# A mean over rows: the first load with 4 rows per partition, as eight DMAs of every eighth partition

## The chip, the cores and the metric

The kernel runs on one core of one Trainium2 chip. The metric is device time in microseconds. Most executions of a kernel agree within 0.3%. A kernel is profiled in one further execution, whose page and trace are quoted below; the durations there are of that execution.

## The reference

```python
batch, seq, dim = 32, 512, 1024
"x": np.random.randn(batch, seq, dim).astype(np.float32),
"divisor": float(dim),

def reference(x, divisor):
    return (np.sum(x, axis=-1) / divisor).astype(np.float32)
```

There are 16384 rows of 1024 float32 values, 67.1 MB; each row gives one mean.

## The kernel before

Each of the 128 partitions of the on-chip memory takes 128 whole rows: 16 from a first block of the input (`x_first`, L150), 96 from a main block (`x_main`), and 16 from a last block (`x_last`). Within a block the rows of one partition are contiguous, so n rows per partition are one piece of n x 4 KB for each partition. The blocks are cut into loads by the lists at L158 to L160. A pair is (rows per partition, how many of these rows ScalarE sums):

- first: 2 rows, then 14, all summed on VectorE
- main: five times 14 rows, then 14 (4 of them on ScalarE) and 12 (5 on ScalarE)
- last: 9, 4 and 2 rows and one row in two halves, `pa` and `pb`

All loads are issued by one engine, SyncE (SP), at L182, in program order, and each is one DMA over all 128 partitions. The tiles `t` of the first and main blocks, and the 9-row tile, rotate through a pool of three buffers (`bulk`, L166). A load into a used buffer waits on SP for the load that filled it and for the sums that read it. VectorE sums a tile with one instruction (L205, `TENSOR_REDUCE`) over all of its rows that aren't ScalarE's; ScalarE takes one row per instruction (L186). GpSimd multiplies the sums by 1/divisor (L207). The last rows are summed one at a time (L192). SP stores three results, at L223, L224 and L228.

Each DMA signals that it has landed on one of eight semaphores, which the framework deals out in turn (101, 102 and 104 to 109 in the trace); the ninth load has the first one's again.

Three helpers edit the finished program. `start_loads_at_once` (L19) takes the loads at the head of SP's list that wait for nothing and puts them into the first block, ahead of the barrier that all engines pass at the entry; it stops at the first load that has a wait. In the kernel before these are three loads: 2, 14 and 14 rows. `latest_wait_first` (L50) sorts the waits of an instruction that has several. `close_while_storing` (L69) lets the closing work run beside the last store.

Of the kernel before, what the change touches and what calls it, by code (L numbers as in the profile page):

```python
# [125 lines left out]
@with_exitstack  # L126
def kernel(
    ctx: ExitStack,
    tc: tile.TileContext,
    x: bass.AP,  # L130
    divisor: float,
    out: bass.AP,
):
    nc = tc.nc
    landed = nc.alloc_semaphore("landed")
    nc.at_finalize(start_loads_at_once)
    nc.at_finalize(latest_wait_first)
    nc.at_finalize(lambda nc: close_while_storing(nc, landed))
    xf = x.flatten_outer_dims()
    N, D = xf.shape  # L140
    P = nc.NUM_PARTITIONS
    scale = 1.0 / float(divisor)
    J = N // P
    assert J * P == N


    F, L = 16, 16
    M = J - F - L
    W = M + L
    x_first = bass.AP(tensor=x.tensor, offset=0, ap=[[F * D, P], [D, F], [1, D]])  # L150
    x_main = bass.AP(tensor=x.tensor, offset=P * F * D, ap=[[W * D, P], [D, M], [1, D]])
    x_last = bass.AP(tensor=x.tensor, offset=P * F * D + M * D, ap=[[W * D, P], [D, L], [1, D]])
    o_first = bass.AP(tensor=out.tensor, offset=0, ap=[[F, P], [1, F]])
    o_main = bass.AP(tensor=out.tensor, offset=P * F, ap=[[W, P], [1, M]])
    o_last = bass.AP(tensor=out.tensor, offset=P * F + M, ap=[[W, P], [1, L]])


    first = [(2, 0), (14, 0)]  # L158
    main = [(14, 0)] * 5 + [(14, 4), (12, 5)]
    last = [(9, 4), (4, 2), (2, 1)]  # L160
    assert sum(n for n, _ in first) == F
    assert sum(n for n, _ in main) == M and sum(n for n, _ in last) == L - 1

    pad = ctx.enter_context(tc.tile_pool(name="pad", bufs=1))
    pad.tile([P, 224], F32, name="pad")
    bulk = ctx.enter_context(tc.tile_pool(name="bulk", bufs=3))  # L166
    one = ctx.enter_context(tc.tile_pool(name="one", bufs=1))
    psum = ctx.enter_context(tc.tile_pool(name="junk", bufs=4, space=bass.MemoryType.PSUM))


    c = 512
    t4 = one.tile([P, 4, D], F32, name="t4")
    t2 = one.tile([P, 2, D], F32, name="t2")
    pa = one.tile([P, 768], F32, name="pa")[:, :c]
    pb = one.tile([P, D - c + 16], F32, name="pb")[:, : D - c + 2]
    res0 = one.tile([P, F], F32, name="res0")
    res = one.tile([P, M], F32, name="res")
    fin = one.tile([P, L], F32, name="fin")
    nc.gpsimd.memset(pb[:, D - c :], 0.0)  # L179

    def load(dst, src):
        tc.keep_in_program_order(nc.sync.dma_start(out=dst, in_=src))  # L182

    def act_sum(dst, src, by=1.0):
        junk = psum.tile([P, D], F32, name="junk")
        nc.scalar.activation(junk, src, COPY, scale=by, accum_out=dst)  # L186

    def dve_mean(dst, src, by=scale):


        h = src.shape[-1] // 2
        nc.vector.tensor_tensor_reduce(  # L192
            out=src[:, :h], in0=src[:, :h], in1=src[:, h:], scale=by, scalar=0.0,
            op0=ADD, op1=ADD, accum_out=dst,
        )

    for loads, src, dst in ((first, x_first, res0), (main, x_main, res)):
        j = 0
        for rows, on_act in loads:
            t = bulk.tile([P, 14, D], F32, name="t")  # L200
            load(t[:, :rows, :], src[:, j : j + rows, :])
            d = rows - on_act
            for i in range(d, rows):
                act_sum(dst[:, j + i : j + i + 1], t[:, i, :])
            nc.vector.reduce_sum(out=dst[:, j : j + d], in_=t[:, :d, :], axis=AX)  # L205
            j += rows
        nc.gpsimd.tensor_scalar_mul(out=dst, in0=dst, scalar1=scale)  # L207
    j = 0
    for rows, on_act in last:
        t = bulk.tile([P, 14, D], F32, name="t")[:, :rows, :] if rows > 4 else t4 if rows == 4 else t2  # L210
        load(t, x_last[:, j : j + rows, :])
        d = rows - on_act
        for i in range(rows):
            if i < d:
                dve_mean(fin[:, j + i : j + i + 1], t[:, i, :])
            else:
                act_sum(fin[:, j + i : j + i + 1], t[:, i, :], by=scale)
        j += rows
    load(pa, x_last[:, j, :c])
    load(pb[:, : D - c], x_last[:, j, c:])  # L220


    tc.keep_in_program_order(nc.sync.dma_start(out=o_first, in_=res0))  # L223
    tc.keep_in_program_order(nc.sync.dma_start(out=o_main, in_=res))  # L224

    dve_mean(pb[:, D - c : D - c + 1], pa, by=1.0)
    dve_mean(fin[:, j:], pb)
    tc.keep_in_program_order(nc.sync.dma_start(out=o_last, in_=fin))  # L228
# [35 lines left out]
```

## Time and profile before

| | |
|---|---|
| median of 3 runs | 160.52 us (160.48 to 160.53) |
| the profiled execution | 160.33 us |
| its span | 159.0 us |
| mean DMA rate over the span | 422 GB/s |
| 14-row load, issue to landing | 35.6 us (median of seven) |
| VectorE sum of 14 rows, 128x14336 | 15.09 us, six times |
| VectorE waits for loads, L205 | 34.0 us in nine waits, the longest 14.6 |

A span runs from the first to the last instruction of the profile, and the execution's own time has 1.33 us around it. The engines are DVE (VectorE), ACT (ScalarE), POOL (GpSimd) and SP (SyncE); a q behind a name is the engine's instruction queue. A row of the timeline has start and duration in us, engine, line, operation, output and input, and in brackets the idle time before it with what ended it. A row of the windows view has a stretch of time, its length, each engine's busy time with instructions, the clock, the busy share of the DMA engines and their rate. The bytes and the time of a packet are counted where the packet begins, so that a rate over a very short stretch can lie above what the engines can do.

### The profile page before, as it was taken

How to read it: one execution, taken by the hardware profiler on the slowest of the kernel's cores; microseconds unless marked ns; L12 is line 12 of the kernel's file. 1: busy time of each engine (PE TensorE's matmuls, PEld its weight loads, DVE VectorE, ACT ScalarE, POOL GpSimd, SP SyncE). 2: the span in 40 equal slices, each digit the busy share in tenths (PEclk: the TensorE clock that was granted, in tenths of full speed). 3: DMA queues.
4: the chain of work that ended last, by engine and by line, in shares of the span. 5: the costliest groups of instructions: out<-in, count | busy, mean ns of one | idle time of the engine just before them, and what ended most of it. 6: DMA issues, size and time to landing. Idle time of an engine off the chain costs nothing.

```text
span 159.0 us, 148 instructions
## 1 busy us (share of the span) xinstructions
DVE 117.2 (74%) x29; ACT 18.5 (12%) x33; POOL 1.0 (1%) x7
## 2 busy tenths in 40 slices
DVE  0500059995999599978999599959995996395643
ACT  3000000000000000000000000000000900390684
POOL 0000000000000000000000000000000000001000
DMA  7999999959999999699999999699999999999894
GB/s 278 447 462 462 462 462 462 462 260 433 462 462 462 462 462 462 303 390 462 462 462 462 462 462 404 303 447 462 462 462 429 396 396 408 482 445 445 350 420 169
DMA packets 2448, 67.18 MB, mean 422 GB/s; under 512 B 656, under 2 KB 656, under 8 KB 912
## 3 DMA queue, kind: packets, MB, share of 16 engines
q1 hardware_dynamic: 2448, 67.18, 98.3%
HBM read 67.11 MB, written 0.07 MB: 422 GB/s over the span
## 4 chain that ended last, share of the span: by engine, by line
DMA 77%; DVE 21%; SPq 1%; issue 0%; DVEq 0%
DMA t<-in_x_dram 56%; DMA pb<-in_x_dram 21%; DVE res L205 20%; SPq L182 1%; DVE pb L192 0%; DVEq L259 0%
## 5 line engine op out<-in xcount | busy, mean ns | idle before, releaser
L205 DVE TENSOR_REDUCE res<-t 128x14 f32<-128x14336 f32 (+3 forms) x9 | 111.2, 12360 | 34.0 <-DMA t<-in_x_dram 34.0
L186 ACT ACTIVATE junk<-t 128x1024 f32<-128x1024 f32 x16 | 16.2, 1013 | 136.8 <-DMA t<-in_x_dram 136.8
L192 DVE CUSTOM_DVE_ANT_0 t<-t 128x512 f32<-128x512 f32 x8 | 5.1, 688 | 6.1 <-DMA t<-in_x_dram 6.1
L186 ACT ACTIVATION_READ_ACCUMULATOR junk<-t 128x1 f32 x16 | 3.0, 186 | 0.0
L207 POOL TENSOR_SCALAR res<-res 128x16 f32<-128x16 f32 (+1 forms) x2 | 0.7, 352 | 143.3 <-DVE res L205 143.3
L186 ACT ACT_TABLE_LOAD x1 | 1.3, 1283 | 1.7 <-PEq L245 1.7
L192 DVE DVE_READ_ACCUMULATOR2_ANT fin<- 128x1 f32 x9 | 0.7, 82 | 0.0
L192 DVE CUSTOM_DVE_ANT_0 pb<-pb 128x257 f32<-128x257 f32 x1 | 0.4, 428 | 0.2 <-DMA pb<-in_x_dram 0.2
L192 DVE CUSTOM_DVE_ANT_0 pa<-pa 128x256 f32<-128x256 f32 x1 | 0.4, 426 | 0.0
L179 POOL MEMSET pb<- 128x2 f32 x1 | 0.1, 99 | 1.3 <-POOLq L245 1.3
L245 POOL MEMSET const-bfloat16-1.0<- 128x1 bf16 x1 | 0.1, 101 | 0.0
L245 POOL MEMSET const-uint8-127<- 128x1 uint8 x1 | 0.1, 101 | 0.0
L245 POOL MEMSET const-float32-0.0<- 128x1 f32 x1 | 0.1, 98 | 0.2 <-issue 0.2
L245 POOL MEMSET const-float32-1.0<- 128x1 f32 x1 | 0.1, 98 | 0.0
L192 DVE DVE_READ_ACCUMULATOR2_ANT pb<- 128x1 f32 x1 | 0.1, 84 | 0.0
## 6 DMA issues: line engine op xcount, KB each, us to landing
t<-in_x_dram SPq DMA_DIRECT2D x7, 7168.0 KB, 35.6
t<-in_x_dram SPq DMA_DIRECT2D x1, 6144.0 KB, 33.3
t<-in_x_dram SPq DMA_DIRECT2D x1, 4608.0 KB, 27.2
t<-in_x_dram SPq DMA_DIRECT2D x2, 1024.0 KB, 19.2
t<-in_x_dram SPq DMA_DIRECT2D x1, 2048.0 KB, 31.7
pa<-in_x_dram SPq DMA_DIRECT2D x1, 256.0 KB, 33.8
pb<-in_x_dram SPq DMA_DIRECT2D x1, 256.0 KB, 33.9
out_dram<-res SPq DMA_DIRECT2D x1, 48.0 KB, 11.6
```

The lines of the kernel that those rows point to most:

```text
L179: nc.gpsimd.memset(pb[:, D - c :], 0.0)
L182: tc.keep_in_program_order(nc.sync.dma_start(out=dst, in_=src))
L186: nc.scalar.activation(junk, src, COPY, scale=by, accum_out=dst)
L192: nc.vector.tensor_tensor_reduce(out=src[:, :h], in0=src[:, :h], in1=src[:, h:], scale=by, scalar=0.0, op0=ADD, op1=ADD, accum_out=dst,)
L205: nc.vector.reduce_sum(out=dst[:, j : j + d], in_=t[:, :d, :], axis=AX)
L207: nc.gpsimd.tensor_scalar_mul(out=dst, in0=dst, scalar1=scale)
L245: nc = _bacc.Bacc("TRN2", target_bir_lowering=False, num_devices=1)
```

## The change

The first load takes 4 rows per partition, and the second 12. The 4-row load is issued as eight DMAs. DMA number e, from 0 to 7, covers partitions e, 8 + e, 16 + e and so on up to 120 + e: sixteen partitions, one piece of 16 KB in each. All eight write the same tile, and VectorE's sum reads it as before. No other load has 4 rows in this loop; the 4-row load of the last block is issued elsewhere.

```diff
-    first = [(2, 0), (14, 0)]
+    first = [(4, 0), (12, 0)]
     main = [(14, 0)] * 5 + [(14, 4), (12, 5)]
     last = [(9, 4), (4, 2), (2, 1)]
...
             t = bulk.tile([P, 14, D], F32, name="t")
-            load(t[:, :rows, :], src[:, j : j + rows, :])
+            if rows == 4:
+
+                for e in range(8):
+                    load(t[e::8, :rows, :], src[e::8, j : j + rows, :])
+            else:
+                load(t[:, :rows, :], src[:, j : j + rows, :])
             d = rows - on_act
```

## The prediction

> **What bounds the kernel now.** I read the page first, for its span, busy shares and queues.
>
> ```profile
> span 159.0 us, 148 instructions
> DVE 117.2 (74%) x29; ACT 18.5 (12%) x33; POOL 1.0 (1%) x7
> q1 hardware_dynamic: 2448, 67.18, 98.3%
> DMA 77%; DVE 21%; SPq 1%; issue 0%; DVEq 0%
> ```
>
> No engine is busy beyond 74%, while the DMA queue's packets fill 98.3% of the sixteen DMA engines' time. The DVE 21% in the chain of waits is a buffer being read before its next load is issued; whether that costs anything is answered by the timeline of DVE.
>
> ```profile
> 4.63 2.29 DVE L205 TENSOR_REDUCE res<-t 128x2 f32<-128x2048 f32 x1 [4.63 <-DMA t<-in_x_dram]
> 21.51 15.09 DVE L205 TENSOR_REDUCE res<-t 128x14 f32<-128x14336 f32 x1 [14.59 <-DMA t<-in_x_dram]
> 38.44 15.09 DVE L205 TENSOR_REDUCE res<-t 128x14 f32<-128x14336 f32 x1 [1.84 <-DMA t<-in_x_dram]
> ...
> 123.10 10.82 DVE L205 TENSOR_REDUCE res<-t 128x10 f32<-128x10240 f32 x1 [1.88 <-DMA t<-in_x_dram]
> ...
> 157.10 0.43 DVE L192 CUSTOM_DVE_ANT_0 pb<-pb 128x257 f32<-128x257 f32 x1 [0.17 <-DMA pb<-in_x_dram]
> ```
>
> Each reduction starts when its tile lands. From 21.51 to 123.10 lie six tiles of 14 rows: 101.59/6 = 16.93 us for 7,340,032 bytes, or 433.5 GB/s, 27.1 per DMA engine. At that rate the input of 67.11 MB takes 154.8 us and the first two rows 2.42. The first tile lands at 4.61, so the stream has an effective start at 4.61 - 2.42 = 2.19; 2.19 + 154.8 = 157.0, and the last piece is indeed summed from 157.10. There is no gap anywhere in the load stream. So each microsecond lost or won by the stream at its start reaches the end, and nothing else does. The start itself is in the windows view and SP's timeline.
>
> ```profile
> core 0: us, DVE busy (x) ACT busy (x) POOL busy (x), PEclk, DMA share, GB/s
> 0.00:1.00 1.00, 0.00 (x0) 0.00 (x0) 0.19 (x4) 1.00 0.00 0
> 1.00:1.25 0.25, 0.00 (x0) 0.00 (x0) 0.00 (x0) 1.00 2.25 360
> 1.25:1.50 0.25, 0.00 (x0) 0.00 (x0) 0.00 (x0) 1.00 0.62 98
> 1.50:1.75 0.25, 0.00 (x0) 0.01 (x1) 0.01 (x1) 1.00 0.43 131
> 1.75:2.00 0.25, 0.00 (x0) 0.25 (x1) 0.09 (x1) 1.00 0.50 197
> 2.00:2.25 0.25, 0.00 (x0) 0.25 (x1) 0.00 (x0) 1.00 0.80 328
> 2.25:2.50 0.25, 0.00 (x0) 0.25 (x1) 0.00 (x0) 1.00 1.16 492
> ```
> ```profile
> 0.00 1.34 SPq L182 DMA_DIRECT2D t<-in_x_dram  x3
> ```
>
> [...]Nothing moves in the first microsecond; the sixteen engines begin between 1.0 and 1.75 us, and the full rate is there only from 2.25. The packet records say the same: first packets begin at 1.02 to 1.68, take 0.31 to 1.01 us where a later 8 KB packet takes 0.309, and the sixteen engines are done with the tile at 3.87 to 4.28; the landing follows 0.33 later. An engine that began at 1.02 and ran at the full rate would be done at 3.44. So the ramp costs the slowest engine 4.28 - 3.44 = 0.84 us: all that the change can win there.
>
> [...]
>
> **The change part by part.** The sum is made on the profiled execution: 160.33 us, span 159.0, 1.33 around it; the median of the runs is 160.52, so 0.19 is added at the end.
>
> *SP's queue.* Seven issues are added ahead of the rest. The three at the start follow each other by some 0.47 us (1.34 for three), so eight end at about 3.8. Eight DMA semaphores are dealt in turn: the second load is the ninth DMA and gets the first one's again. The store at L224, in the same position in the kernel before, has an event wait of its own on the load that last had its semaphore, so I expect the second load to wait for the first small DMA, the third load for the second. A load with a wait is not moved to the start by L19, so it comes after the entry barrier: 0.33 us after the last early issue in before (1.34 to the barrier's end at 1.67), so here at about 4.1, its packets at 5.1 to 5.8. The small DMAs keep the engines fed till 5.9 at least (1.02 + 4.84), so this is hidden; if the stream were faster by a microsecond it would show. Behind SP in the barrier wait the ACT table load (1.74) and a memset: first needed at 123 and 157 us, nothing.
>
> *The packets.* Each engine gets eight packets of 16 KB and eight of 48 KB where it had eight of 8 KB and eight of 56 KB: as many, the same bytes. Seven more semaphore packets at 6 ns each in the packet records: +0.04. Small DMAs queued one behind the other cost nothing more by themselves: pb lands 33.9 + 123.14 = 157.04, pa 33.8 + 122.64 = 156.44, 0.60 for 256 KB, the full rate.
>
> *DVE.* Reductions cost 1.067 us a row and 0.15 each (from 15.09 for 14 and 2.29 for 2): 4.42 for 4 rows, 12.95 for 12, together as before. It sat idle 14.59 us in this stretch. The buffer of tile 0 comes free later, but its next load's bytes aren't due before 38 us. Nothing.
>
> *The ramp.* With one packet per engine in the first DMA the engines could all begin near 1.02 and the loss of 0.84 shrink. But first packets that began late (1.55 to 1.68) were done at about the same moment as the early ones, 2.0[...]. From 0 to 0.8 gained; I take 0.4.
>
> [...] Lower bound nothing[...]; upper bound half the rate: the 2.10 MB last 9.67 us and not 4.84, +4.84. [...] I take +4.84[...].
>
> Sum: +4.84 + 0.04 - 0.4 = +4.5; 160.33 + 4.5 = 164.8, on the median's scale **165.0**.
>
> **The rivals.**
>
> *A, [...] 165.0, from 163.8 to 166.0.* [...] Against: no trace here shows it.
>
> *B, not slower.* [...] Its place is the first 5 us[...]. Then only the ramp counts: -0.8 to 0, +0.04; at 0.4 gained, 159.97 + 0.19 = 160.2, best case 159.8. For it: the slow start is real[...].
>
> *C, the change doesn't do what it says.* If a DMA on these partitions reached only eight of the engines, the others would begin with the fifth DMA, 4 x 0.47 = 1.9 us later, and end late by that: +1.9 + 0.04 - 0.4 = +1.5, 162.1. The same size comes out if each 16 KB packet pays some 0.2 us anew[...]: 7 x 0.2 + 0.04 = 1.4. The pa and pb landings speak against the latter[...].
>
> **How the numbers follow.** A 0.66, C 0.10, B 0.24. The limit of telling from no change is 0.2%, 0.32 us. B divides at a gain of 0.32: 0.16 faster, 0.08 within. Faster 0.16, same 0.08, slower 0.76. For the range, B's faster part (0.16) and a tail above A are left out: 160.2 to 166.0; A's own is 163.8 to 166.0.
>
> **What would show it.** In the profile after: A has the first reduction (128x4) start near 11.5 (1.02 + 9.67 + 0.33, and some 0.4 of ramp) and some 217 GB/s up to 10 us; the second (128x12) near 26; then 16.93 per tile as before, and every later start 4.5 later. B has 6.3 to 7.0 for the first reduction, C about 8.5. The ninth load should be issued at about 4.1 us. I am wrong if the first reduction starts before 9 us; wrong in another way if it starts at 11.5 and the end doesn't move, for then the stream had slack that I deny.

## The result and the profile after

| | before | after |
|---|---|---|
| median | 160.53 us | 165.23 us (165.10 to 165.28) |
| profiled execution, span | 160.33, 159.0 us | 165.28, 163.9 us |

The ratio is 1.0292, with a 95% interval from 1.0274 to 1.0309: slower by 4.70 us. One execution of e5 (187.86 us) and one of e6 (188.53 us, the profiled one) below fell in a slower state of the chip; they are left out of the medians, and no trace of e6 is read. Of the page after, these lines answer to those of before: the span, DVE's busy time, the DMA queue and the chain of waits.

```profile
span 163.9 us, 161 instructions
DVE 117.3 (72%) x29; ACT 18.5 (11%) x33; POOL 1.0 (1%) x7
q1 hardware_dynamic: 2560, 67.18, 98.1%
DMA 74%; DVE 21%; SPq 3%; issue 0%; DVEq 0%
```

DVE does the same work. The DMA engines still count as busy for 98.1% of a span that is 4.9 us longer, with the same 67.18 MB. The DMA engines are not waiting somewhere, then: packets take longer. The busy share alone would hide that. The timeline of DVE after shows where (L210 here is L205 of before):

```profile
12.50 4.42 DVE L210 TENSOR_REDUCE res<-t 128x4 f32<-128x4096 f32 x1 [12.50 <-DMA t<-in_x_dram]
26.64 12.95 DVE L210 TENSOR_REDUCE res<-t 128x12 f32<-128x12288 f32 x1 [9.73 <-DMA t<-in_x_dram]
43.53 15.09 DVE L210 TENSOR_REDUCE res<-t 128x14 f32<-128x14336 f32 x1 [3.93 <-DMA t<-in_x_dram]
...
127.98 10.82 DVE L210 TENSOR_REDUCE res<-t 128x10 f32<-128x10240 f32 x1 [1.80 <-DMA t<-in_x_dram]
...
162.03 0.43 DVE L192 CUSTOM_DVE_ANT_0 pb<-pb 128x257 f32<-128x257 f32 x1 [0.22 <-DMA pb<-in_x_dram]
```

The second reduction covers the first sixteen rows in both kernels: it starts at 26.64 and not at 21.51, 5.13 late. The last sum is 4.93 late (162.03 against 157.10). All of the loss is there when sixteen rows are loaded, and almost all of it reaches the end. The windows view of the kernel after has the rate of those first microseconds:

```profile
core 0: us, DVE busy (x) ACT busy (x) POOL busy (x), PEclk, DMA share, GB/s
0.00:1.00 1.00, 0.00 (x0) 0.00 (x0) 0.19 (x4) 1.00 0.00 0
1.00:2.00 1.00, 0.00 (x0) 0.00 (x0) 0.00 (x0) 1.00 0.90 262
2.00:4.00 2.00, 0.00 (x0) 0.00 (x0) 0.00 (x0) 1.00 1.14 254
4.00:6.00 2.00, 0.00 (x0) 0.35 (x1) 0.10 (x1) 1.00 0.93 197
6.00:8.00 2.00, 0.00 (x0) 0.93 (x1) 0.00 (x0) 1.00 1.01 221
8.00:10.00 2.00, 0.00 (x0) 0.00 (x0) 0.00 (x0) 1.00 1.12 229
```

From 2 to 10 us the DMA share is about 1 at some 225 GB/s, about half of the steady 433.5. Sixteen engines are at work, each at half its rate. They don't wait for SP's issues either, as the chain of waits shows:

```profile
3.78 0.59 SPq L182
...
4.41 7.96 DMA t<-in_x_dram
```

The last of the eight DMAs is issued from 4.41 us on (start, duration, what), and it lands 7.96 us after that.

### The profile page after: what moved, and what is told of

It is laid out like the page before. It is cut to its first block, busy times and chain, and to the rows that moved or that the text cites. A ratio compares the mean times of both kernels' runs of the same rounds, so it can differ in the third digit from the quotient of the medians.

```text
span 163.9 us, 161 instructions
## 1 busy us (share of the span) xinstructions
DVE 117.3 (72%) x29; ACT 18.5 (11%) x33; POOL 1.0 (1%) x7
## 2 busy tenths in 40 slices
DMA packets 2560, 67.18 MB, mean 410 GB/s; under 512 B 768, under 2 KB 768, under 8 KB 1024
## 3 DMA queue, kind: packets, MB, share of 16 engines
q1 hardware_dynamic: 2560, 67.18, 98.1%
## 4 chain that ended last, share of the span: by engine, by line
DMA 74%; DVE 21%; SPq 3%; issue 0%; DVEq 0%
DMA t<-in_x_dram 53%; DVE res L210 21%; DMA pb<-in_x_dram 21%; SPq L182 3%; DVE pb L192 0%; DVEq L210 0%; DVEq L264 0%
## 5 line engine op out<-in xcount | busy, mean ns | idle before, releaser
L210 DVE TENSOR_REDUCE res<-t 128x14 f32<-128x14336 f32 (+4 forms) x9 | 111.2, 12360 | 38.9 <-DMA t<-in_x_dram 38.9
## 6 DMA issues: line engine op xcount, KB each, us to landing
t<-in_x_dram SPq DMA_DIRECT2D x2, 6144.0 KB, 27.1
```

## The experiments

Each edit is against the changed kernel. P stands for the explanation by the destination: how fast a DMA's packets go depends on which partitions it writes, and on which the DMA before it wrote. How much each set of partitions takes in was the author's assumption; no trace of before shows it. P's forecasts are 175.1 us for e2, 163.0 for e3, 163.4 for e4, 165.2 for e5, 170.4 for e6 and 173.4 for e10. The rivals are the source addresses (sixteen pieces 512 KB apart, read in step), SP's issue, and a fixed price for each small DMA.

The plainest sign is in the trace's packet records: how long a 16 KB packet takes. The table gives medians of sixteen packets at a time in order of their start, in us, for the eight groups of the 4-row load's 128 packets; each row has the label of a run below. The first group, at the head of these DMAs, differs from the rest in every run and isn't compared.

```
                      1     2     3     4     5     6     7     8
e1_one_dma          1.10  0.61  0.61  0.61  0.61  0.61  0.61  0.61
changed kernel      0.88  1.08  1.26  1.27  1.09  1.24  1.27  1.26
e2_sixteen_in_a_row 1.26  2.08  2.09  2.09  2.09  2.09  2.09  2.09
e3_all_ports_half   0.95  0.61  0.93  0.62  0.89  1.21  1.09  1.20
e4_sides_in_turn    0.93  1.01  1.07  1.07  1.09  1.09  1.09  1.09
e5_source_neighb.   0.88  1.17  1.25  1.26  1.08  1.23  1.26  1.26
e7_every_fourth     1.15  0.61  0.61  0.62  0.61  0.61  0.61  0.61
e8_every_second     1.04  0.61  0.62  0.61  0.61  0.61  0.61  0.61
e9_twelve_then_four 0.77  1.25  1.28  1.28  1.07  1.23  1.28  1.28
e10_row_same_side   1.30  2.41  2.10  2.41  2.11  2.41  2.10  2.41
```

**e1_one_dma: the rows without the split.**

```diff
-                for e in range(8):
-                    load(t[e::8, :rows, :], src[e::8, j : j + rows, :])
+                load(t[:, :rows, :], src[:, j : j + rows, :])
```

> Undoes the split alone: 4 rows and then 12, but the 4-row load is one DMA over all 128 partitions. Every theory that puts the loss on the eight DMAs expects the time before, 160.5 (160.3 to 160.8), and the first reduction at about 7.0 us. If the row counts (4 and 12) cost anything themselves, it is 161 or more.

Measured: 160.50 us, ratio 0.9993 (0.9985 to 1.0002). Its windows view, for the same stretches:

```profile
core 0: us, DVE busy (x) ACT busy (x) POOL busy (x), PEclk, DMA share, GB/s
2.00:4.00 2.00, 0.00 (x0) 1.01 (x1) 0.00 (x0) 1.00 0.98 418
4.00:6.00 2.00, 0.00 (x0) 0.00 (x0) 0.00 (x0) 1.00 0.99 426
6.00:8.00 2.00, 0.95 (x1) 0.00 (x0) 0.00 (x0) 1.00 1.06 459
```

Packets of the same size are twice as fast at the same DMA share. The row counts cost nothing; the whole loss belongs to the eight DMAs.

**e2_sixteen_in_a_row: neighbouring partitions.**

```diff
-                    load(t[e::8, :rows, :], src[e::8, j : j + rows, :])
+                    load(t[16 * e : 16 * e + 16, :rows, :], src[16 * e : 16 * e + 16, j : j + rows, :])
```

> Eight DMAs of sixteen neighbouring partitions (0 to 15, 16 to 31, ...) in place of every eighth. [...] a 16 KB packet takes about 2.4 us and the 2.10 MB 19.3 us; the end is 14.5 us after that of the kernel before, 175.1. Source addresses (sixteen pieces 512 KB apart read in step are slow, neighbouring ones 64 KB apart are not): no loss, 160.5 to 161. Issue (SP's 0.63 us for each small DMA sets the pace): the same as the changed kernel, 165.2.

Measured: 172.00 us, ratio 1.0710 (1.0681 to 1.0740). The windows view of this run:

```profile
core 0: us, DVE busy (x) ACT busy (x) POOL busy (x), PEclk, DMA share, GB/s
4.00:6.00 2.00, 0.00 (x0) 1.28 (x1) 0.10 (x1) 1.00 1.00 123
6.00:8.00 2.00, 0.00 (x0) 0.00 (x0) 0.00 (x0) 1.00 1.07 131
```

Issue and source addresses are out as the cause: the number of DMAs is the same, SP issues them faster (one every 0.46 us and not every 0.63), the pieces lie closer together in memory, and the loss is 11.45 us where it was 4.70. But P had said 175.1: packets take 2.09 us and not 2.4. e4 and e10 take that up.

**e3_all_ports_half: sixteen partitions four apart, then 32 in a row.**

```diff
-                for e in range(8):
-                    load(t[e::8, :rows, :], src[e::8, j : j + rows, :])
+                for e in range(32, 36):
+                    load(t[e : e + 61 : 4, :rows, :], src[e : e + 61 : 4, j : j + rows, :])
+                for e in (0, 96):
+                    load(t[e : e + 32, :rows, :], src[e : e + 32, j : j + rows, :])
```

> The 4-row load is four DMAs of sixteen partitions four apart between 32 and 95[...], and then two DMAs of 32 partitions, 0 to 31 and 96 to 127[...]. [...] the first four run at the full rate, packets of 0.61 to 0.7 us, 2.4 us for the half of the bytes; the others at the half rate, packets of 1.26, 4.9 us; the end is 2.4 to 2.6 after before, 163.0. A cost of small DMAs with one packet per engine as such: the first four are as slow as in the changed kernel, and the last two are fast. Source addresses: pieces are 256 KB and 64 KB apart, no loss, 160.5.

Measured: 165.16 us (164.33 to 165.59), ratio 1.0273 (1.0236 to 1.0309). The time missed the 163.0 of P: as much is lost as in the changed kernel. The packets bear P out in part. Of the four groups with sixteen partitions four apart, the second and the fourth have medians of 0.61 and 0.62, so a small DMA isn't slow as such; 32 partitions in a row give 1.09 to 1.21 in the last three. But the third group has 0.93, which P doesn't explain.

Two things are in the packet records that P's sum left out. The sixteen engines come out unequal: they reach the second load between 8.96 and 10.52 us, where in e1 they do between 6.31 and 6.69. The slowest is 3.83 us behind e1's, and the span 4.0 us longer (163.0 against 159.0). And the engines stand idle at times: from 3 to 6 us they are busy 84% of the time, where in the changed kernel they have no gap to speak of. SP issues these DMAs 0.63 us apart, no faster than the engines move them at 0.61, so they may have waited for SP here. That wasn't tested, nor why the engines become unequal. Why other executions of this kernel lie up to 1.3 us above the profiled one (164.33) stays open too.

**e4_sides_in_turn: the same DMAs, another order.**

```diff
-                for e in range(8):
+                for e in (0, 4, 1, 5, 2, 6, 3, 7):
```

> The same eight DMAs in the order 0, 4, 1, 5, 2, 6, 3, 7[...]. [...] in the changed kernel the packets around its only change fell from 1.26 to 1.08 us. With seven changes in place of one, some 0.3 us each, 163.4. Source addresses, issue, or a cost per small DMA: no difference of order, 165.2.

Measured: 164.31 us, ratio 1.0228 (1.0206 to 1.0249). Order matters, as of the explanations above only P says (164.31 us against 165.23): it gives back 0.9 us of the 1.8 that P expected. Packets are at 1.07 to 1.09 from the third group on, the value that the changed kernel has behind the head (group 2, 1.08) and in group 5 (1.09), where e goes from 3 to 4.

**e5_source_neighbours: the destination kept, the source changed.**

```diff
-                    load(t[e::8, :rows, :], src[e::8, j : j + rows, :])
+                    load(t[e::8, :rows, :], src[16 * e : 16 * e + 16, j : j + rows, :])
```

> Destination partitions as in the changed kernel (every eighth), but each of the eight DMAs reads sixteen pieces that are neighbours in memory, 64 KB apart and not 512 KB; the first block's means of these 4 rows so land at permuted places, and the amount of work is the same. [...] only the destination counts, 165.2 (164.9 to 165.6), packets of 1.26 us, first reduction near 12.5. Source addresses: full rate, 160.5 to 161.

Measured: 165.30 us, ratio 1.0295 (1.0274 to 1.0317), with the packets of the changed kernel. Of source and destination, only the destination counts here.

**e6_eight_rows: twice the bytes in the eight DMAs.**

```diff
-    first = [(4, 0), (12, 0)]
+    first = [(8, 0), (8, 0)]
...
-            if rows == 4:
+            if rows == 8 and j == 0:
```

> The first load takes 8 rows per partition and the second 8, so each of the eight DMAs has packets of 32 KB. [...] the loss goes with the bytes, packets of 2.4 to 2.5 us, 19.6 us for what takes 9.7 at the full rate: 160.5 + 9.9 = 170.4, less perhaps half a microsecond. A fixed price for each of the eight DMAs (its issue, its semaphore, an engine that starts anew): the same loss as with 4 rows, 165.2, or less where the packets hide it.

Measured: 170.94 us, ratio 1.0644 (1.0621 to 1.0667). The loss is 10.4 us for 4.2 MB and 4.7 for 2.1 MB: it goes with the bytes, a little more than in proportion. A fixed price per DMA or per packet is out: the number of both is the same.

**e7_every_fourth and e8_every_second: more partitions in each DMA.**

```diff
-                for e in range(8):
-                    load(t[e::8, :rows, :], src[e::8, j : j + rows, :])
+                for e in range(4):
+                    load(t[e::4, :rows, :], src[e::4, j : j + rows, :])
```

e8 has `range(2)` and a step of 2.

> The 4-row load is four DMAs of every fourth partition: 32 partitions[...], and two packets per engine. [...] this has the full rate: 160.5, with some 0.3 more for a later first packet, 160.8. If an engine takes two partitions that are next to each other in the list, [...] 164.3, like the run with the sides in turn.

> The 4-row load is two DMAs of every second partition: 64 partitions[...], four packets per engine. [...] 160.5 to 160.8. Packets dealt in the order of the list: 8 consecutive partitions of the tile per engine in the end[...], between 164.3 and 165.2.

Measured: e7 161.87 us, ratio 1.0087 (1.0064 to 1.0111); e8 160.85, ratio 1.0015 (1.0008 to 1.0022). Packets are at 0.61 in both, as in e1: DMAs of 32 partitions four apart and of 64 two apart lose nothing in the medians behind the first group. Why is not shown. e7 lies between its two cases; in its packet records some packets that begin near 4.6 us take up to 1.75 us, and I have not tested why. e8 is the clean case of the split without slow packets, and its windows view shows what remains:

```profile
core 0: us, DVE busy (x) ACT busy (x) POOL busy (x), PEclk, DMA share, GB/s
0.00:1.00 1.00, 0.00 (x0) 0.00 (x0) 0.19 (x4) 1.00 0.00 0
1.00:2.00 1.00, 0.00 (x0) 0.00 (x0) 0.00 (x0) 1.00 0.87 229
2.00:4.00 2.00, 0.00 (x0) 1.08 (x1) 0.10 (x1) 1.00 0.89 377
```

Up to 4 us it is behind e1 (418 GB/s from 2 to 4). Its first packet begins at 1.34 us and not at 1.00. Here the split by steps over partitions makes the start later, not earlier.

**e9_twelve_then_four: the eight DMAs behind the 12-row load.**

```diff
-    first = [(4, 0), (12, 0)]
+    first = [(12, 0), (4, 0)]
```

> The 12-row load comes first, as one DMA over 128 partitions, and the eight DMAs of the 4-row load behind it: [...] the start of the stream is that of the kernel before. If the changed kernel's first packets, one per engine, won 0.4 us of the ramp as the forecast has it, this loses that again and is slower than it: 165.6. If its start was later by the 0.34 us that its first packet came later, this one is faster: 164.9. If the loss came from the start[...], it is near 160.5.

Measured: 165.58 us, ratio 1.0316 (1.0299 to 1.0333). The windows view of this run:

```profile
core 0: us, DVE busy (x) ACT busy (x) POOL busy (x), PEclk, DMA share, GB/s
2.00:16.00 14.00, 0.00 (x0) 1.28 (x1) 0.10 (x1) 1.00 0.91 393
16.00:18.00 2.00, 0.64 (x1) 0.00 (x0) 0.00 (x0) 1.00 1.11 279
18.00:20.00 2.00, 2.00 (x1) 0.00 (x0) 0.00 (x0) 1.00 1.01 205
```

The slow stretch moves with the DMAs, to 16 us and later; it isn't a matter of the start. The loss is 5.07 us (165.58 - 160.51) where the changed kernel loses 4.70. The difference of 0.37 has the size forecast for the ramp, but the two intervals of the ratio overlap, so it is indicated and not settled.

**e10_row_same_side: e2 in another order.**

```diff
-                for e in range(8):
+                for e in (0, 2, 1, 3, 4, 6, 5, 7):
                     load(t[16 * e : 16 * e + 16, :rows, :], src[16 * e : 16 * e + 16, j : j + rows, :])
```

> Sixteen neighbouring partitions per DMA as in the run that gave 172.0, in the order 0, 2, 1, 3, 4, 6, 5, 7[...]. [...] at the four places without a change the packets stay at 2.4 to 2.5 us where they were at 2.09, some 0.35 us each, 173.4. [...] the order doesn't matter: 172.0.

Measured: 173.21 us, ratio 1.0790 (1.0774 to 1.0806). The packets alternate between 2.41 us in the second DMA of each pair (0 and 2, 1 and 3, 4 and 6, 5 and 7) and 2.10 in the first of the next pair. In e2's order, where no DMA follows its partner, all are at 2.08 or 2.09. So how fast a DMA's packets go depends on the partitions of the DMA before it, too, against the forecast of 172.0. Why is not shown; the records don't say which engine a packet is on. And 2.41 us for 16 KB is 6.8 GB/s for each engine, 109 for sixteen: a quarter of the steady 433.5.

No version was faster than the kernel before; e1 is level with it.

## Why the prediction was right

- **No slack in the load stream.** Right. 5.13 us late at sixteen rows, 4.93 at the end. The 0.2 in between comes back at 0.04 per tile: the 14-row tiles follow each other by (127.98 - 43.53)/5 = 16.89 us, before by 16.93.
- **Half the rate, +4.84.** That the loss goes with the destination partitions is shown by e2, e5 and e10 against addresses and issue, and by e6 against a price per DMA. Half the rate was the author's assumption: before has no DMA on fewer than 128 partitions and doesn't show it. The runs gave 0.61 us for a 16 KB packet with all 128 partitions (e1), 1.26 with every eighth, 2.41 with sixteen in a row (e10). The size was a little low: with e9 this term and the seven semaphore packets come to 5.07, where the sum had 4.88. A packet takes 1.26 us and not 1.21 (twice 16 KB at 27.1 GB/s), less what group 5 gives back (1.09). And the slow stretch doesn't end with the 4-row load: the first 48 KB packet of each engine takes 2.35 us (median) where it takes 1.81 in e1, which the sum didn't have. Why it does wasn't tested. The semaphore packets were misread: 9 ns each in the records of before, and up to 25 in the slow stretch, not 6; for seven that is 0.18 us at most, where the sum had 0.04.
- **Ramp, -0.4.** The size agrees with the 0.37 of e9, so far as that can tell, but by luck: the reason given does not hold. The engines did not all begin near 1.02: the packet records have their first packets from 1.36 to 1.79, where before the first began at 1.02. Where the packets are at the full rate, e8, the split lost 0.29 us (160.85 against 160.56). Why the eight DMAs cost less at the head (4.70) than behind the 12-row load (5.07, e9), if they do, wasn't tested.
- **SP's queue.** The second load is issued at 5.65 us, not at 4.1. Its wait for the first small DMA is there, as argued from L224, and was met by then. Most of the lateness comes from the small DMAs: 0.63 from one to the next instead of 0.47, so that the eight end at 5.0 and not at 3.8. The rest is the barrier, which took 0.6 after them and not 0.33. The cover held, because the engines were busy with the first load until 10.4. At the full rate it would hardly have held, by an estimate: in e1 the engines take up the second load at 6.3 to 6.7 us, and a load issued at 5.65 has its first packets about a microsecond later (1.00 in e1).
- **First reduction at 11.5.** It came at 12.50. In the packet records the last engine is through with the first load at 11.45, and the landing comes 0.93 us after that, not 0.33 as in e1 (6.69 and 7.02) and as the forecast took it from before. Why it takes longer is open. That delay stays local: the second reduction is at 26.64 where about 26 was forecast, and the end of the profile is 4.93 late where 4.5 was forecast.
- **The rivals.** B (not slower) falls with e2 and e5: the same sixteen engines with the same bytes, and the time goes with the destination partitions. C in its first form (eight engines only) falls with the packet records: sixteen packets have begun by 1.79 us, the first of each engine. Its second form (each packet pays 0.2 us anew) falls with e6, where as many packets of twice the size lose over twice as much.

## What to carry to other kernels

Before a DMA is split by partitions, measure the parts. Here the same sixteen engines took 0.61 us for 16 KB with all 128 partitions (e1) and with 32 or 64 in steps (e7, e8), 1.08 to 1.27 with every eighth partition (changed kernel) and 2.08 to 2.41 with sixteen in a row (e2, e10), all as medians, and the busy share of the DMA engines stayed near 1 all the same (e2: 1.00 at 123 GB/s). In a stream without slack, what is lost at the head is lost at the end (5.13 us at sixteen rows, 4.93 at the end). If the parts must be every eighth partition, the order 0, 4, 1, 5, 2, 6, 3, 7 takes back some of it (164.31 us against 165.23). And one DMA over all 128 partitions lost nothing (e1).

## What was not expected of the hardware

- The issue of a DMA whose partitions are stepped takes SP longer than that of one with neighbouring partitions: 0.589 us against 0.420 for sixteen partitions (changed kernel and e2, trace), and its first packet comes 0.34 later (1.36 against 1.02). With a source that isn't stepped the issue takes as long (0.589, e5), so it is the step of the destination that seems to count.
- DMAs of sixteen partitions in a row moved no more than a quarter of the steady 433.5 GB/s (16384/2.41 x 16 = 109) in e10's slow groups, and every eighth partition a little less than half of it (16384/1.265 x 16 = 207 in the changed kernel).
- The DMA behind the eight starts at a lower rate as well: 2.35 us against 1.81 for an engine's first 48 KB packet (changed kernel and e1), 2.76 after e2's DMAs; the second such packet is at 1.81 again in all three.
